# Two ordering edges in the gemm pairs of a gated streaming-encoder block: sums of the next pair's weights behind y22, the cast of its first weights behind the copy of x12

## The chip, the cores and the metric

The kernel runs on one core of a Trainium2 chip. The metric is the device time of one execution in microseconds (us), smaller being better; the time shown is the median of three runs. In the profile PE is TensorE (matmuls), PEld its weight loads, DVE is VectorE, ACT ScalarE, POOL GpSimd and SP SyncE, the engine that issues most of the DMAs. "SPq" is SP's DMA queue.

## The reference, cut to what matters

One layer, 1024 tokens of width 1024, all in float32. The change touches the first matrix product only, the input projection; everything behind it reads what that writes.

```python
D_MODEL = 1024
BATCH = 1
SEQ = 1024
DEPTH = 1
...
h = rmsnorm(x, norm_g[l])
proj = h @ w_in[l]
q, k, v, za, u, vs, zs, gm = jnp.split(proj, IN_SPLITS, axis=-1)
q = partial_rope(q.reshape(B, S, ATT_HEADS, HEAD_DIM), pos)
k = partial_rope(k.reshape(B, S, ATT_KV_HEADS, HEAD_DIM), pos)
...
a = window_sink_attention(q, k, v, att_sinks[l])
a = (a * jax.nn.silu(za)) @ w_att_out[l]
sgo = chunked_spatial_gating(jax.nn.gelu(u, approximate=False),
                             jax.nn.gelu(vs, approximate=False),
                             sg_w[l], sg_b[l], sg_ln_g[l], sg_ln_b[l])
sgo = (sgo * jax.nn.silu(zs)) @ w_sg_out[l]
ga, gs = jnp.split(jax.nn.sigmoid(gm + b_merge[l]), N_BRANCHES, axis=-1)
y = ga * a + gs * sgo
x = x + y @ w_o[l]
return rmsnorm(x, final_g)
```

## The kernel before, in words

**A product.** A float32 product is made from two halves of each factor: a "hi" in the rounded type fp32r and a "lo", the rest. `split` makes them: ScalarE casts the hi (L189), VectorE subtracts it from the source for the lo (L190). `product` then runs hi·hi, hi·lo and lo·hi for each of four blocks of the inner dimension: 12 matmuls of 128x512 into one bank (L410). The lo of a weight is therefore wanted by the third matmul of the product that uses it.

**A gemm pair.** The columns of the weights are worked off in pairs of 128-column blocks. `gemm_pair` makes one pair's result, four quarters of 128x512, from seven products in place of eight, with sums of the weights and of the activations in the factors. The forms of the activations (b11, t1, t2, b21, t3, b22, t4) are made once per stage; the forms of the weights are made for each pair:

- the first weights, unit (n, 0), of which only 512 columns are cast in pairs 0 to 5;
- the sums sa, units (n, 2) and (n, 3), two additions (L299, L300) of raw weights on VectorE, then a cast and a lo over 1024 columns;
- the sums sb, units (n, 4) and (n, 5), two more additions (L296, L297), then the same;
- the last weights, unit (n, 6).

The products are written in the order b11, t1, t2, b21, t3, b22, t4; the scheduler puts some matmuls of b22 ahead of t3. For pairs 0 to 5 (`IN_HEAD`) the b21 product is made earlier, in the head of the kernel, and written to DRAM (`made_dr`); `split_next` loads it into the free half of the first weights' hi buffer (`wh`), and VectorE adds it at L447 in place of a product. Until L447 has run, that buffer is not free.

Between the products the bank of b11, t2, t3 and t4 (`ps_mm`) and the bank of t1 and b22 (`ps_o`) are read out:

- x11 is ScalarE's copy of b11 (L444), and L447 completes it;
- x22 begins with ScalarE's negated copy of t1 (L458), which empties `ps_o` for b22;
- x12 is ScalarE's copy of the bank behind t2 (L461); t3 goes on in the same bank;
- y22 is x22 less the bank behind t3 (VectorE, L473); t4 goes on in the bank behind it;
- x12 is completed by the bank of b22 (VectorE, L477);
- the last quarter is ScalarE's copy of the bank behind t4.

`finish` sends each quarter on. Pairs 0 to 3 make U, pair 4 the keys and values, pairs 5 to 8 the queries Q. In the Q pairs each quarter is split again (`split_q`: ScalarE's L1344, VectorE's two L1346, called a qhl pair in the prediction) and stored on SP as `q_hl` (L1349), and its raw value as `q_raw` (L571). Pair 4's values go through a transpose and a cast and lo of `vt` (ScalarE, VectorE).

**Where the weights of the next pair come from.** `split_next`, called four times in a pair, takes the next unit of a list. It runs one pair ahead: the first weights of pair n+1 are cast, its sums made and its loads asked for while pair n is multiplied. Raw weights come through three `wr` buffers, hi and lo through three `wh` and `wl` buffers each, sums through two `s` buffers. A pair needs two raw buffers; each is loaded by DMAs on SP's queue (`copy_to`, L241), in the Q pairs four of 128 KB for each buffer. A load waits until the last reader of the buffer's old content is done, and what stands behind it on SP waits as well.

**What sets the order.** The program is written in one sequence; a scheduler then lays each engine's instructions in one row, following the data and its own costs, and an engine works off its row in order. `after(second, first)` adds an edge that only orders two instructions in that row: on one engine, it costs no semaphore. `make_sums(first)` passes such an edge to the first addition of each sum, where one is given; `behind_of` holds it by pair and has no entry for pairs 1 to 6 before the change.

Of the kernel before, what the change touches and what calls it, by code (L numbers as in the profile page):

```python
# [54 lines left out]
def hybrid_tile(  # L55
# [16 lines left out]
    nc = tc.nc  # L72
# [109 lines left out]
    def split(hi, lo, src, minus=False):  # L182
        if minus:
            nc.scalar.mul(hi, src, -1.0)
            return nc.vector.scalar_tensor_tensor(
                lo, src, -1.0, hi.bitcast(F32), op0=ALU.mult, op1=ALU.subtract
            )
        else:
            hi_casts.append(nc.scalar.copy(hi, src))  # L189
            return nc.vector.tensor_sub(lo, src, hi.bitcast(F32))  # L190

    def after(second, first):

        tc.add_manual_dep(
            second.ins,
            first.ins.name,
            mybir.DependencyInfo(mybir.DependencyClass.NoSync, mybir.DependencyReason.DATA),
            reason="order",
        )
# [49 lines left out]
    def split_next(hold=False):  # L249

        if not units:
            begin_job()
        if not units:
            return
        halves, keys = units.pop(0)
        if keys[0][1] == 2 and not locked[0]:
            make_sums(behind_of.get(keys[0][0]))
        if callable(halves):
            halves = halves()
        hi = mtile([P, D], F32R, "wh", 3)  # L260
        lo = mtile([P, D], F32R, "wl", 3)
        if isinstance(halves, list):
            for c, half in enumerate(halves):
                split(hi[:, half_of(c)], lo[:, half_of(c)], half)
        else:
            wide = halves.shape[1]
            if hold:
                nc.scalar.copy(hi[:, 0:wide], halves)
                for c, key in enumerate(keys):
                    ready[key] = hi[:, half_of(c)], lo[:, half_of(c)]  # L270
                return lambda: nc.vector.tensor_sub(lo[:, 0:wide], halves, hi[:, 0:wide].bitcast(F32))
            first = split(hi[:, 0:wide], lo[:, 0:wide], halves)
            splits.append(first)
            if keys[0] == (done[0] - 1, 6) and done[0] > LAST_OF_Q + 2 and not locked[0]:
                make_sums(first)
        for c, key in enumerate(keys):
            ready[key] = hi[:, half_of(c)], lo[:, half_of(c)]
        n = keys[0][0]
        if keys == [(n, 0)] and n in IN_HEAD:
            ready[n, 1] = hi[:, HALF:D].bitcast(F32)  # L280
            copy_to(ready[n, 1], made_dr[n])
        if len(units) == 1 and not locked[0]:
            begin_job()
# [22 lines left out]
        return [lambda at=at: made[at][:] for at in range(2)]  # L306

    loads_of = []
    IN_HEAD = range(6)

    def make_sums(first=None, most=2):
# [116 lines left out]
    def mark(copy):  # L428
        if not by_products[0]:
            pace[0] = copy  # L430

    def gemm_pair(b, finish, hook=lambda: None, second="o", begun=None, last_form=None):

        n = done[0]
        done[0] += 1
        if begun:
            acc = begun.pop(0)
        else:  # L440
            acc = bank("mm")[:]
            product(acc, ready[n, 0], b["b11"], True)
        x11, x12, x22 = xtile(), xtile(), xtile()
        mark(nc.scalar.copy(x11[:], acc))  # L444

        def first_term(t2):
            term[0] = nc.vector.tensor_add(x11[:], x11[:], t2)  # L447
            finish(0, 0, x11, x11[:], 1.0)

        if n in IN_HEAD:  # L450
            first_term(ready[n, 1])
        hook()
        if begun:
            t5 = begun.pop(0)
        else:
            t5 = bank("o")[:]
            product(t5, ready[n, 2], b["t1"], True)
        mark(nc.scalar.mul(x22[:], t5, -1.0))  # L458
        hook()
        product(acc, ready[n, 3], b["t2"], False)  # L460
        mark(nc.scalar.copy(x12[:], acc))  # L461
        split_next()
        hook()
        if n not in IN_HEAD:
            t2 = bank(second)[:]
            product(t2, ready[n, 1], b["b21"], True)
            first_term(t2)
        split_next()
        if last_form:
            last_form()  # L470
        hook()
        product(acc, ready[n, 4], b["t3"], False)
        term[0] = nc.vector.tensor_sub(x22[:], x22[:], acc)  # L473
        finish(1, 1, x22, x22[:], 1.0)
        hook()
        product(t5, ready[n, 5], b["b22"], False)
        term[0] = nc.vector.tensor_add(x12[:], x12[:], t5)  # L477
        finish(0, 1, x12, x12[:], 1.0)
        split_next()
        hook()  # L480
        product(acc, ready[n, 6], b["t4"], False)
        finish(1, 0, xtile(), acc, -1.0)
        split_next()
        hook()
# [755 lines left out]
    for m in range(0, KC, 2):  # L1240
        last_u[0] = m == KC - 2

        def finish(i, half, q, src, sign, m=m):
            nc.scalar.activation(q[:], src, AF.Gelu, scale=sign)
            late.append(lambda: mix(m + i, half, q))
# [215 lines left out]
    keys = {}  # L1461
# [968 lines left out]
```

## Time and profile before

| | before |
|---|---|
| device time, median of 3 runs | 900.67 us (897.28, 900.67, 901.84) |
| the profiled execution, device time | 894.7 us |
| its span in the profile | 892.3 us |
| granted TensorE clock, mean | 0.997 |
| ScalarE busy | 559.4 us (63%) |
| GpSimd busy | 164.4 us (18%) |
| DMA | 216.99 MB, mean 243 GB/s |
| HBM, read and written | 280 GB/s over the span |

TensorE's and VectorE's rows stand in the prediction. The profiled execution is one of its own, 6.0 us below the median of the timed runs; the span is the time from its first to its last recorded instruction.

In a row of the timeline the columns are: start in us from the beginning of the span, duration in us, engine, line, operation, output<-inputs (names without their buffer numbers), shapes and types, and in brackets the idle time of the engine just before, with what ended it. In the list of waits a row gives engine, tile and line of the one that waits, engine, tile and line of the one that releases it, then the sum of the idle time, the count, and the mean. In a table of windows a row gives the stretch, its length, then for PE, PEld, DVE, ACT, POOL and SP the busy time with its count, then the mean granted clock, the busy share of the DMA engines and the GB/s that they moved.

### The profile page before, as it was taken

The numbers are of one execution on the slowest core, as the hardware profiler recorded it, in microseconds if no ns is written. First come the engines' busy times: TensorE is split into PE (matmuls) and PEld (weight loads), VectorE is DVE, ScalarE is ACT, GpSimd is POOL, SyncE is SP. The second block draws the span as 40 slices with busy tenths as digits, with TensorE's granted clock in tenths as the row PEclk, the third lists the DMA queues.
The fourth block names the chain that finished last, engine by engine and source line by source line (L and its number), as shares of the span: only waits on it lengthen the run. The fifth ranks groups of instructions, "written<-read, shape, count | busy, mean of one in ns | idle before, by whom it ended". The sixth has DMA issues, their size and how long they took to land.

```text
span 892.3 us, 13261 instructions
## 1 busy us (share of the span) xinstructions
PE 882.3 (99%) x4131; PEld 731.1 (82%) x4131; DVE 698.0 (78%) x1354; ACT 559.4 (63%) x1097; POOL 164.4 (18%) x267
## 2 busy tenths in 40 slices
PE   9999999999999999999999999999999999999996
PEld 5888888887888888888888888888888888888885
DVE  7876697764687779888889887654898699579986
ACT  7775564333455468889888886443585485467543
POOL 3112311123021012323322210122201111110013
PEclk9999999999999999999999999999999999999998
DMA  9977867769788879999999994889869568998533
GB/s 326 230 205 205 210 143 172 184 213 279 254 284 264 275 238 249 262 339 278 269 340 295 269 285 127 307 302 261 229 186 358 191 193 266 284 261 274 184 123 114
DMA packets 134630, 216.99 MB, mean 243 GB/s; under 512 B 13372, under 2 KB 62144, under 8 KB 134560
## 3 DMA queue, kind: packets, MB, share of 16 engines
q1 hardware_dynamic: 111736, 152.50, 52.8%
q0 software_dynamic: 22672, 63.45, 29.4%
q8 instruction: 33, 0.54, 0.2%
q14 instruction: 37, 0.30, 0.1%
q10 hardware_dynamic: 152, 0.20, 0.1%
HBM read 157.77 MB, written 91.88 MB: 280 GB/s over the span
## 4 chain that ended last, share of the span: by engine, by line
PE 96%; DMA 2%; issue 1%; DVE 1%; SPq 0%; DVEq 0%; ACT 0%; ACTq 0%; POOLq 0%
PE ps_mm L410 46%; PE ps_o L410 25%; PE ps_tp L410 4%; PE ps_sc L410 3%; PE ps_sc L716 3%; PE ps_o L716 2%; PE ps_two L1584 2%; PE ps_tp L1214 2%; PE ps_o L1721 2%; PE ps_tp L1659 2%; PE ps_mm L716 2%; PE ps_tp L716 1%; PE ps_o L1729 1%; DMA wr<-in_x_dram 1%; PE ps_tp L1671 1%
## 5 line engine op out<-in xcount | busy, mean ns | idle before, releaser
L189 ACT CAST wh<-s 128x1024 fp32r<-128x1024 f32 (+1 forms) x66 | 65.7, 998 | 68.5 <-issue 22.1
L190 DVE TENSOR_TENSOR wl<-wr,wh 128x512 fp32r<-128x512 f32 (+1 forms) x63 | 56.0, 890 | 64.8 <-ACT wh L189 62.5
L189 ACT CAST wh<-wr 128x512 fp32r<-128x512 f32 (+1 forms) x63 | 49.2, 782 | 59.0 <-PE ps_mm L410 32.4
L190 DVE TENSOR_TENSOR wl<-s,wh 128x1024 fp32r<-128x1024 f32 (+1 forms) x66 | 76.1, 1155 | 9.4 <-ACT wh L189 8.6
L362 POOL DMA_DIRECT2D sums<-in_w_dram x48 | 35.1, 737 | 170.7 <-PE ps_mm L410 94.1
L410 PE MATMUL ps_o<-T_b22h,wh 128*128 128x512 f32 x148 | 58.2, 394 | 0.9 <-ACT x L458 0.9
L410 PE MATMUL ps_o<-T_t1h,wh 128*128 128x512 f32 x148 | 58.5, 396 | 0.0
L410 PE MATMUL ps_o<-T_t1h,wl 128*128 128x512 f32 x148 | 57.9, 391 | 0.0
L410 PE MATMUL ps_o<-T_b22h,wl 128*128 128x512 f32 x148 | 57.8, 391 | 0.0
L410 PE MATMUL ps_o<-T_t1l,wh 128*128 128x512 f32 x148 | 57.7, 390 | 0.0
L410 PE MATMUL ps_o<-T_b22l,wh 128*128 128x512 f32 x148 | 57.7, 390 | 0.0
L1631 ACT ACTIVATE pr<-pr,sm 128x193 f32<-128x193 f32 (+2 forms) x128 | 55.9, 439 | 1.7 <-DVE sm L1615 1.0
L410 PE MATMUL ps_mm<-T_t4h,wh 128*128 128x512 f32 (+1 forms) x144 | 56.4, 392 | 0.0
L410 PE MATMUL ps_mm<-T_t3h,wh 128*128 128x512 f32 x140 | 55.7, 398 | 0.0
L410 PE MATMUL ps_mm<-T_t4h,wl 128*128 128x512 f32 (+1 forms) x144 | 55.5, 385 | 0.0
L410 PE MATMUL ps_mm<-T_t4l,wh 128*128 128x512 f32 (+1 forms) x144 | 55.4, 385 | 0.0
L410 PE MATMUL ps_mm<-T_b11h,wh 128*128 128x512 f32 x140 | 55.0, 392 | 0.0
L410 PE MATMUL ps_mm<-T_t3h,wl 128*128 128x512 f32 x140 | 54.7, 391 | 0.0
L410 PE MATMUL ps_mm<-T_t3l,wh 128*128 128x512 f32 x140 | 54.7, 390 | 0.0
L410 PE MATMUL ps_mm<-T_b11l,wh 128*128 128x512 f32 x140 | 54.7, 390 | 0.0
L410 PE MATMUL ps_mm<-T_b11h,wl 128*128 128x512 f32 x140 | 54.6, 390 | 0.0
L410 PE MATMUL ps_mm<-T_t2h,wl 128*128 128x512 f32 x140 | 54.6, 390 | 0.0
(512 smaller groups left out, 2537.0 us busy)
## 6 DMA issues: line engine op xcount, KB each, us to landing
wr<-in_w_dram SPq DMA_DIRECT2D x80, 256.0 KB
sums<-in_w_dram POOLq DMA_DIRECT2D x24, 512.0 KB, 6.2
s<-sums SPq DMA_DIRECT2D x24, 512.0 KB
q_hl<-qhl SPq DMA_DIRECT2D x16, 512.0 KB
q<-q_hl SPq DMA_DIRECT2D x64, 128.0 KB
wr<-in_w_dram SPq DMA_DIRECT2D x15, 512.0 KB
y_dr<-x POOLq DMA_DIRECT2D x28, 256.0 KB, 6.1
sums<-in_w_dram POOLq DMA_DIRECT2D x24, 256.0 KB, 7.1
```

Of the source, the lines that this page charges most:

```text
L189: hi_casts.append(nc.scalar.copy(hi, src))
L190: return nc.vector.tensor_sub(lo, src, hi.bitcast(F32))
L362: return lambda: paced(nc.gpsimd.dma_start(dst, src, accum_op=op))
L410: mm = nc.tensor.matmul(acc, lt, rt, start=fresh and k == 0 and n == 0, stop=k == 3 and n == 2, skip_group_check=True,)
L716: mm = nc.tensor.matmul(acc, lt, rt, start=first and n == 0, stop=last and n == 2, skip_group_check=True)
L1214: nc.tensor.matmul(pm[:, t * P : (t + 1) * P], xh[:, half * 4 + t, g * P : (g + 1) * P], bias[-1][1][:, g % 2, :], start=True, stop=True,)
L1584: nc.tensor.matmul(st.sc[:, i], q_of[:, c, i * P : (i + 1) * P], kt[:, :, lo:hi], start=True, stop=True)
L1631: nc.scalar.activation(v, v, AF.Exp, bias=st.nmax[:, c, i : i + 1], scale=-1.0, accum_out=st.sums[:, c, i : i + 1])
L1659: nc.tensor.transpose(st.inner[0 : P if st.t else 64, at : at + P], st.pr[:, i, place_of(c, 64 if st.t else P, 192)], ident[:],)
L1671: nc.tensor.transpose(st.ends[0:wide, i * P : (i + 1) * P], st.pr[:, i, 129 : 129 + wide], ident[:])
L1721: nc.tensor.matmul(st.po[:], lt, rt, start=i == 0, stop=False, skip_group_check=True)
L1729: nc.tensor.matmul(st.po[:, cols(c)], ends[:, c, vs], st.b[:, cols(c)], start=False, stop=c == 1, skip_group_check=True)
```

## The change: what it does

Three edits, all of order; no instruction is added or taken away.

1. In `split_next`, the cast of pair n+1's first weights is ordered behind pair n's copy of x12 (L461), if that copy was kept.
2. In `gemm_pair`, that copy is kept in `copies` for pairs 0 to 5.
3. In `gemm_pair`, y22's subtraction (L473) of pairs 0 to 5 is put into `behind_of` for the next pair, so that the four additions of pair n+1's sums are ordered behind it.

```diff
@@ split_next
             first = split(hi[:, 0:wide], lo[:, 0:wide], halves)
+            if keys[0][1] == 0 and keys[0][0] - 1 in copies:
+                after(hi_casts[-1], copies[keys[0][0] - 1])
             splits.append(first)
@@
     loads_of = []
+    copies = {}
     IN_HEAD = range(6)
@@ gemm_pair
         product(acc, ready[n, 3], b["t2"], False)
-        mark(nc.scalar.copy(x12[:], acc))
+        second_copy = nc.scalar.copy(x12[:], acc)
+        mark(second_copy)
+        if n in IN_HEAD:
+            copies[n] = second_copy
         split_next()
@@
         product(acc, ready[n, 4], b["t3"], False)
         term[0] = nc.vector.tensor_sub(x22[:], x22[:], acc)
+        if n in IN_HEAD:
+            behind_of[n + 1] = term[0]
         finish(1, 1, x22, x22[:], 1.0)
```

The lines behind the edits move down: L447 is L450 after the change, L458 L461, L461 L464, L473 L479, L477 L485, the additions L299, L300, L296, L297 are L301, L302, L298, L299, and L1344, L1346, L1349, L571 are L1352, L1354, L1357, L579, and L410 L413.

Below are the rows at three places, before and after, as the program lays them (line, operation, output<-inputs, shape; the first number in a name counts tiles).

VectorE, from the end of pair 4 to y22 of pair 5, before. `s_321` and `s_322` are the sums of pair 6, made of its raw weights `wr_305` and `wr_306`; `s_299` is the first sum of pair 5; `x_310` is x11, `x_312` x22 of pair 5; `wh_293` holds the product made in the head for it.

```order
L190 TENSOR_TENSOR khl_297_1935<-x_287_1846,khl_297_1935 128x512
L299 TENSOR_TENSOR s_321_2095<-wr_306_1972 128x512
L190 TENSOR_TENSOR wl_304_1968<-s_299_1945,wh_303_1967 128x1024
L300 TENSOR_TENSOR s_321_2095<-s_321_2095,wr_305_1971 128x512
L296 TENSOR_TENSOR s_322_2098<-wr_305_1971,wr_306_1972 128x512
L190 TENSOR_TENSOR vt_308_1986<-ps_tp_307_1981,vt_308_1986 128x8x64
L447 TENSOR_TENSOR x_310_2011<-x_310_2011,wh_293_1891 128x512
L297 TENSOR_TENSOR s_322_2098<-wr_305_1971,s_321_2095 128x512
L190 TENSOR_TENSOR wl_316_2050<-wr_282_1804,wh_315_2049 128x512
L190 TENSOR_TENSOR wl_318_2054<-wr_305_1971,wh_317_2053 128x1024
L1346 SCALAR_TENSOR_TENSOR qhl_313_2017<-x_310_2011,qhl_313_2017 128x256 x2
L473 TENSOR_TENSOR x_312_2013<-x_312_2013,ps_mm_309_1998 128x512
```

VectorE after, the same place up to the last lo ahead of y22.

```order
L190 TENSOR_TENSOR khl_297_1935<-x_287_1846,khl_297_1935 128x512
L190 TENSOR_TENSOR wl_304_1968<-s_299_1945,wh_303_1967 128x1024
L190 TENSOR_TENSOR vt_308_1986<-ps_tp_307_1981,vt_308_1986 128x8x64
L450 TENSOR_TENSOR x_310_2011<-x_310_2011,wh_293_1891 128x512
L190 TENSOR_TENSOR wl_316_2050<-wr_282_1804,wh_315_2049 128x512
L190 TENSOR_TENSOR wl_318_2054<-wr_305_1971,wh_317_2053 128x1024
```

And the rows that follow these, from y22 (L479 now) to the lo of pair 6's first sum, `wl_324`; `qhl_319` is the split of y22, `qhl_320` that of x12 (`x_311`).

```order
L479 TENSOR_TENSOR x_312_2013<-x_312_2013,ps_mm_309_1998 128x512
L301 TENSOR_TENSOR s_321_2095<-wr_306_1972 128x512
L1354 SCALAR_TENSOR_TENSOR qhl_313_2017<-x_310_2011,qhl_313_2017 128x256 x2
L1354 SCALAR_TENSOR_TENSOR qhl_319_2071<-x_312_2013,qhl_319_2071 128x256 x2
L485 TENSOR_TENSOR x_311_2012<-x_311_2012,ps_o_314_2022 128x512
L302 TENSOR_TENSOR s_321_2095<-s_321_2095,wr_305_1971 128x512
L298 TENSOR_TENSOR s_322_2098<-wr_305_1971,wr_306_1972 128x512
L1354 SCALAR_TENSOR_TENSOR qhl_320_2090<-x_311_2012,qhl_320_2090 128x256 x2
L299 TENSOR_TENSOR s_322_2098<-wr_305_1971,s_321_2095 128x512
L190 TENSOR_TENSOR wl_324_2102<-s_321_2095,wh_323_2101 128x1024
```

All four additions have moved from ahead of L473 (three of them from ahead of L447) to behind it; pair 5's own `wl_304` and the `vt` of pair 4 have moved up.

ScalarE in pair 5, before; `wh_315` is the hi of pair 5's last weights, `wh_317` that of pair 6's first weights, `wh_323` that of pair 6's first sum, `x_311` x12.

```order
L444 COPY x_310_2011<-ps_mm_309_1998 128x512
L189 CAST wh_315_2049<-wr_282_1804 128x512
L458 ACTIVATE x_312_2013<-ps_o_314_2022 128x512
L189 CAST wh_317_2053<-wr_305_1971 128x1024
L461 COPY x_311_2012<-ps_mm_309_1998 128x512
L1344 ACTIVATE qhl_313_2017<-x_310_2011 128x4x2x64
```

And after:

```order
L447 COPY x_310_2011<-ps_mm_309_1998 128x512
L189 CAST wh_315_2049<-wr_282_1804 128x512
L461 ACTIVATE x_312_2013<-ps_o_314_2022 128x512
L464 COPY x_311_2012<-ps_mm_309_1998 128x512
L189 CAST wh_317_2053<-wr_305_1971 128x1024
L1352 ACTIVATE qhl_313_2017<-x_310_2011 128x4x2x64
```

One swap: the cast of `wh_317` now stands behind the copy of x12.

TensorE at the same place, from the last matmul of t2 to the first of t3, before. `ps_o_314` is the bank of t1 and b22 in pair 5, `ps_mm_309` the other; `wh_303` and `wl_304` are pair 5's second sum.

```order
L410 MATMUL ps_mm_309_1998<-T_t2h_128_708,wl_301_1949 128x512
L410 MATMUL ps_o_314_2022<-T_b22h_79_448,wh_303_1967 128x512
L410 MATMUL ps_o_314_2022<-T_b22l_80_449,wh_303_1967 128x512
L410 MATMUL ps_o_314_2022<-T_b22h_79_448,wl_304_1968 128x512
L410 MATMUL ps_o_314_2022<-T_b22h_79_448,wh_303_1967 128x512
L410 MATMUL ps_o_314_2022<-T_b22l_80_449,wh_303_1967 128x512
L410 MATMUL ps_o_314_2022<-T_b22h_79_448,wl_304_1968 128x512
L410 MATMUL ps_o_314_2022<-T_b22h_79_448,wh_303_1967 128x512
L410 MATMUL ps_mm_309_1998<-T_t3h_138_792,wh_303_1967 128x512
```

And after:

```order
L413 MATMUL ps_mm_309_1998<-T_t2h_128_708,wl_301_1949 128x512
L413 MATMUL ps_o_314_2022<-T_b22h_79_448,wh_303_1967 128x512
L413 MATMUL ps_o_314_2022<-T_b22l_80_449,wh_303_1967 128x512
L413 MATMUL ps_o_314_2022<-T_b22h_79_448,wl_304_1968 128x512
L413 MATMUL ps_o_314_2022<-T_b22h_79_448,wh_303_1967 128x512
L413 MATMUL ps_mm_309_1998<-T_t3h_138_792,wh_303_1967 128x512
```

Three of the seven b22 matmuls ahead of t3 have moved behind it; four stay. In pairs 1 and 3 one moves so, in pair 4 two.

SP from the loads of pair 7 on, before; `wr_329` and `wr_330` are pair 7's raw buffers, `qhl_313`, `qhl_319`, `qhl_320` and `qhl_326` the four quarters of pair 5.

```order
L241 DMA wr_329_2129<-in_w_dram 128x2x128 x4
L241 DMA wr_330_2130<-in_w_dram 128x2x128 x4
L1319 DMA rot_335_2156<-in_cos_dram 128x128
L1320 DMA rot_335_2156<-in_sin_dram 128x128
L1349 DMA q_hl_95<-qhl_313_2017 128x2x512
L571 DMA q_raw_94<-x_312_2013 128x512
L571 DMA q_raw_94<-x_311_2012 128x512
L1349 DMA q_hl_95<-qhl_319_2071 128x2x512
L1349 DMA q_hl_95<-qhl_320_2090 128x2x512
L571 DMA q_raw_94<-x_325_2117 128x512
L1349 DMA q_hl_95<-qhl_326_2120 128x2x512
```

And after:

```order
L241 DMA wr_329_2129<-in_w_dram 128x2x128 x4
L1327 DMA rot_335_2156<-in_cos_dram 128x128
L1328 DMA rot_335_2156<-in_sin_dram 128x128
L579 DMA q_raw_94<-x_312_2013 128x512
L1489 DMA v_488_3075<-v_dr_98 64x2x192
L1357 DMA q_hl_95<-qhl_313_2017 128x2x512
L1357 DMA q_hl_95<-qhl_319_2071 128x2x512
L579 DMA q_raw_94<-x_311_2012 128x512
L1357 DMA q_hl_95<-qhl_320_2090 128x2x512
L579 DMA q_raw_94<-x_325_2117 128x512
L1357 DMA q_hl_95<-qhl_326_2120 128x2x512
L241 DMA wr_330_2130<-in_w_dram 128x2x128 x4
```

The four loads of `wr_330` have moved from behind those of `wr_329` to behind the last store of pair 5.

## The prediction

> **What bounds the kernel now.** First the page's totals, the clock and the chain that ended last.
>
> ```profile
> span 892.3 us, 13261 instructions
> PE 882.3 (99%) x4131; PEld 731.1 (82%) x4131; DVE 698.0 (78%) x1354; ACT 559.4 (63%) x1097; POOL 164.4 (18%) x267
> PEclk9999999999999999999999999999999999999998
> PE 96%; DMA 2%; issue 1%; DVE 1%; SPq 0%; DVEq 0%; ACT 0%; ACTq 0%; POOLq 0%
> ```
>
> TensorE is the bound: 99% busy, at full granted clock, 96% of the chain. An edit that moves only vector, scalar and DMA work can gain what TensorE waits, or cost new waits, and nothing else. So the second view is the waits of TensorE alone, over the whole span; this is all of it.
>
> ```profile
> PE ps_o L629 <- DVE T_b22l L117: 1.5, 1, 1.5
> PE ps_o L410 <- ACT x L458: 0.9, 1, 0.9
> PE ps_mm L811 <- ACT T_t2h L735: 0.6, 1, 0.6
> ```
>
> Two of the three lie in the first 13 us, ahead of all gemm pairs. One, 0.9 us, lies among the pairs that the diff touches. The timeline places it: first TensorE around it.
>
> ```profile
> 212.85 0.39 PE L410 MATMUL ps_o<-T_t1h,wh 128*128 128x512 f32 x1
> ...
> 217.38 0.39 PE L410 MATMUL ps_mm<-T_t2h,wl 128*128 128x512 f32 x1
> 218.62 0.50 PE L410 MATMUL ps_o<-T_b22h,wh 128*128 128x512 f32 x1 [0.86 <-ACT x L458]
> ...
> 224.39 0.50 PE L410 MATMUL ps_mm<-T_t4h,wh 128*128 128x512 f32 x1
> 224.73 0.40 PE L410 MATMUL ps_mm<-T_t4l,wh 128*128 128x512 f32 x1
> ```
>
> This is pair 5, the first Q pair. From 212.85 to 217.38 are 20 steps, so a step is 0.2265 us. After its t2 product TensorE stands until ScalarE has read t5 (L458). ScalarE and VectorE tell why it is late.
>
> ```profile
> 208.91 1.05 ACT L189 CAST wh<-s 128x1024 fp32r<-128x1024 f32 x1 [0.71 <-PE ps_mm L410]
> ...
> 211.21 0.59 ACT L189 CAST vt<-ps_tp 128x512 fp32r<-128x512 f32 x1 [0.74 <-PE ps_tp L1286]
> 212.35 0.59 ACT L444 COPY x<-ps_mm 128x512 f32<-128x512 f32 x1 [0.56 <-PE ps_mm L410]
> 217.46 0.62 ACT L189 CAST wh<-wr 128x512 fp32r<-128x512 f32 x1 [4.51 <-DVE x L447]
> 217.98 0.59 ACT L458 ACTIVATE x<-ps_o 128x512 f32<-128x512 f32 x1
> 218.47 1.04 ACT L189 CAST wh<-wr 128x1024 fp32r<-128x1024 f32 x1
> 219.41 0.59 ACT L461 COPY x<-ps_mm 128x512 f32<-128x512 f32 x1
> ```
>
> ```profile
> 204.21 0.69 DVE L473 TENSOR_TENSOR x<-x,ps_mm 128x512 f32<-128x512 f32 x1 [2.86 <-PE ps_mm L410]
> ...
> 213.19 0.69 DVE L299 TENSOR_TENSOR s<-wr 128x512 f32<-128x512 f32 x1 [3.91 <-DMA wr<-in_w_dram]
> 213.80 1.22 DVE L190 TENSOR_TENSOR wl<-s,wh 128x1024 fp32r<-128x1024 f32 x1
> 214.94 0.68 DVE L300 TENSOR_TENSOR s<-s,wr 128x512 f32<-128x512 f32 x1
> ...
> 216.74 0.68 DVE L447 TENSOR_TENSOR x<-x,wh 128x512 f32<-128x512 f32 x1
> ...
> 223.66 0.68 DVE L473 TENSOR_TENSOR x<-x,ps_mm 128x512 f32<-128x512 f32 x1
> ```
>
> VectorE sat 3.91 us at the first sum of pair 6 (L299), whose weights had not landed. Behind it stood L447 of pair 5, which frees the wh buffer for ScalarE's cast at 217.46, which stands ahead of L458. So TensorE's wait comes from a sum that nobody needed yet.
>
> **The change, part by part.** Instructions are the same in kind and number; only order changes.
>
> *The sums of pair 6 go behind y22 (L473) of pair 5.* Then, from these rows: VectorE's lo part of s (1.14 a step) follows the cast that ends at 209.96, and ends by 211.2; that of vt follows its cast and ends at 212.4; L447 follows the copy that ends at 212.94, and is done at 213.6 instead of 217.4. The cast takes 0.62, and L458 then waits only for t1's end, about 215.1: done at 215.7, and TensorE asks at 217.38 + 0.23 = 217.61. The 0.86 us is gone, with 1.9 us to spare. What is late next is the x12 copy (L461): t3 needs it.
>
> *The cast of pair 6's first weights goes behind that copy.* The copy then starts when t2 ends, 217.38 + 0.39, and ends at about 218.4; four b22 matmuls, which the new order leaves ahead of t3, cover until 217.61 + 4 × 0.2265 = 218.52. No wait, 0.1 us spare. The moved cast (1.04) is done by 219.4 and wanted at 225.8. In pairs 0 to 4 the same swap has no wait of TensorE to remove (the list above is complete), and the casts have spare time of the same kind: I count them at nothing. If the copy's cover is gone, a pair loses about 0.1 us.
>
> The sums of pairs 2 and 5 move as well, and their products come later still.
>
> ```profile
> 144.07 0.69 DVE L473 TENSOR_TENSOR x<-x,ps_mm 128x512 f32<-128x512 f32 x1 [2.27 <-PE ps_mm L410]
> 153.89 0.39 PE L410 MATMUL ps_o<-T_t1h,wh 128*128 128x512 f32 x1
> ```
>
> From L473 at 144.07, four steps of 0.60 (the third is L477), a mixing step of 0.67, the cast of 1.05 and the lo of 1.2 end by 149.4; t1 of pair 2 starts at 153.89. For pair 5 the same count from 204.21 ends by 209.6; its t1 starts at 212.16, three steps ahead of 212.85. Both cost nothing; if that cover were gone, each would cost the 1.2 of its lo.
>
> *The gain.* From 217.38 to 224.39 TensorE makes 25 steps in 7.01 us; at 0.2265 they take 5.66. TensorE's start of t4 had also to wait for L473 at 223.66, so its first step took 0.34 for 0.23: in all **1.45 us**.
>
> *What the moved sums release later.* Each raw buffer is read by sums and then refilled on SP's queue, so its loads move too.
>
> ```profile
> 203.49 4.32 SPq L241 DMA_DIRECT2D wr<-in_w_dram  x5
> 218.83 5.95 SPq L241 DMA_DIRECT2D wr<-in_w_dram  x8
> 226.04 0.38 SPq L1349 DMA_DIRECT2D q_hl<-qhl  x1
> 207.20 5.43 DMA wr<-in_w_dram
> 229.16 0.67 ACT L1344 ACTIVATE qhl<-x 128x512 fp32r<-128x512 f32 x1 [0.34 <-DMA q_hl<-qhl]
> 250.36 0.36 SPq L1349 DMA_DIRECT2D q_hl<-qhl  x1
> ```
>
> The fourth row is from the chain: the last load of the group of five landed 5.43 us after its issue at 207.20, and its sum started at 213.19, 6.0 after. The fifth gives 3.1 us from the issue of a store at 226.04 to its first user. These are my two ends, from issue to use.
>
> Pair 6's second buffer now waits for the last sum of pair 5. Behind L473 at 204.21 come six steps of 0.60, so that sum ends at 208.5; two small stores go out first, then four loads of 0.86, the last at 211.5: in use by 217.5 at the latest, and its sum stands at 221.9. Hidden, 4 us spare. From there VectorE's queue (the order in front shows it; steps of 0.60, 0.67 for a qhl pair, 1.14 for a lo) reaches the lo of pair 6's first s at 227.0 to 228.2. t1 of pair 6 wants it at 217.61 + 48 × 0.2265 + 0.45 = 228.9. Hidden, 0.7 us spare.
>
> Pair 7's second buffer is the tight one. Its four loads went out in the eight from 218.83; now they stand on SP behind four stores of q_hl, the last of which waits for VectorE: after 228.2 a small copy, a lo and a qhl pair, so 230.1. Four issues of 0.74: the last at 232.8, in use from 235.9 or 238.8. VectorE's sums of pair 7 wait for it, and they are not held behind anything: ahead of L447 and L473 of pair 6 they stand as they did before at pair 5. VectorE is held until 235.2 anyway, by a lo whose cast waits for t2. TensorE's next starts of t4 are:
>
> ```profile
> 244.49 0.39 PE L410 MATMUL ps_mm<-T_t4h,wh 128*128 128x512 f32 x1
> 263.53 0.39 PE L410 MATMUL ps_mm<-T_t4h,wh 128*128 128x512 f32 x1
> ```
>
> Pair 6's t4 needs L473, and is due at 244.49 - 1.45 = 243.04. From the first use, three sums, L447, a sum, a lo, a qhl pair and L473 take 1.8 + 0.6 + 0.6 + 1.14 + 0.67 + 0.69 = 5.5: L473 ends at 241.4 or 244.3. A wait of 0 or **1.3 us**; it begins with a first use after 237.5. To choose, the bytes in that stretch:
>
> ```profile
> q_hl<-qhl SPq DMA_DIRECT2D x9, 512.0 KB
> wr<-in_w_dram SPq DMA_DIRECT2D x24, 128.0 KB
> q_raw<-x SPq DMA_DIRECT2D x9, 256.0 KB
> 225.00:235.00 10.00, 10.00 (x46) 8.27 (x45) 8.23 (x21) 4.77 (x8) 0.00 (x0) 1.00 0.92 329
> 235.00:245.00 10.00, 10.00 (x50) 8.29 (x49) 5.00 (x9) 4.91 (x8) 0.00 (x0) 1.00 0.59 184
> ```
>
> Four q_hl, four q_raw and the four loads are 3.67 MB; at 329 GB/s (the last column of the first stretch) 11.2 us from 222.5, so 233.7, ahead of the last issue plus 3.1. I take the lower end, no wait, and keep 1.3.
>
> The Trainium skill, DMA: Bandwidth & Descriptors, section Anatomy of one DMA, fits one copy at about 2.0 us plus bytes over 436 GB/s, 2.3 us for 128 KB. By that the last load lands at 235.1 and the sum stays 1.45; by the row's 5.43 and the 0.56 behind it the gain is all but lost. The trace has 5.43 where the page would have 2.3.
>
> Pair 8's last load goes behind pair 7's last q_hl store in the same way: issued at 250.36 + 0.36 - 1.45 = 249.3, in use from 252.4 or 255.3. From there four sums and a short lo, L447, a rotation, a lo, a qhl pair, a rotation and L473 (3.0 + 0.6 + 0.6 + 1.14 + 0.67 + 0.6 + 0.69) take 7.3: L473 of pair 7 ends at 259.7 or 262.6, and t4 is due at 263.53 - 1.45 = 262.08: 0 or **0.5 us**, and again I take the lower end. After that the orders agree but for one step.
>
> *The sum.* 892.3 - 1.45 = 890.85 of span; the profiled execution, with the 2.4 us around its span, goes from 894.7 to 893.25. The median of the three timed runs is 900.67, 6.0 above the profiled one; less 1.45 it is **899.2**. With both upper ends, 1.8, the sum is +0.35 and the median 901.0.
>
> **The rivals.** *The wait moves to pair 6 (slower).* If pair 7's loads come later than the rows say, the same stall is made anew: each us after 237.5 is one lost, and from 238.95 on the change loses. For it: the five loads took 213.19 - 203.49 = 9.7 us from first issue to use; 9.7 from 230.6 is 240.3, a wait of 2.8. Pair 8's load, 1.5 us later than its upper end in the same way, adds 0.5 + 1.5 = 2.0. Sum -1.45 + 4.8 = +3.35: 904.0. Against it: they ran against POOL's stores of k and v, and the two stretches above have none (POOL 0.00), the second with the DMA engines 0.59 busy. [...]
>
> *The gain is larger.* Timed runs lie 2.6 to 7.1 us above the profiled one (897.28 and 901.84 against 894.7). Where a load lands later, the old order loses one for one and the new has 4 us spare. If a third of the median's 6.0 is this wait, the gain is 3.5: 897.2. Against it: nothing shows where those 6 us are.
>
> *The change does not do what it says.* L447 still comes after 216.2, since something else holds VectorE, and L458 with it: 900.7. The rows above leave 2.6 us against that.
>
> **How the numbers follow.** Forecast 899.2 (its own range 899.2 to 901.0): 0.66. Slower, 904.0: 0.14. Larger gain, 897.2: 0.13. No effect, 900.7: 0.07. The range goes from the fastest run less the gain, 897.28 - 1.45 = 895.8, to 902.9, half way from the slowest run with no gain, 901.84, to the slower rival; half of that rival and the far tail of the larger gain stay outside. About what a measurement of this kernel can tell from no change is 0.5%, 4.5 us: below 896.2 only by the tail of the larger gain, 0.06; above 905.2 only by a landing far beyond the rival's, 0.04; the rest 0.90.
>
> **What would show it.** Right: TensorE's list of waits has no L458; L447 of pair 5 starts near 213.0; ScalarE's copy L461 of pair 5 near 217.8; t4 of pair 6 near 243.0. Wrong: a wait of TensorE on y22 in pairs 6 or 7, VectorE idle at the first sum of pair 7 beyond 237.5, a wait on the x12 copy in any pair, or TensorE's time lost in a stretch that no moved row touches.

## The result: 893.5 us, and a profile that hardly moved

| | before | after |
|---|---|---|
| device time, median of 6 runs each | 900.36 us (896.12 to 901.84) | 893.47 us (892.65 to 893.88) |
| ratio after to before | | 0.993, 95% interval 0.9906 to 0.9955 |
| the profiled execution, device time | 894.7 us | 893.83 us |
| its span | 892.3 us | 892.0 us |

The change makes the kernel 6.9 us faster by the medians, about 6 us by the ratio (0.7% of 900, 0.45 to 0.94%). The forecast was 899.2 with a range from 895.8: too little by 5.7 us, and the time lies outside the range. Yet the spans of the two profiles differ by 0.3 us, and the runs of after lie within 1.2 us, those of before within 5.7. The question is thus not only where the time went, but why the profile of before did not have it.

First the profile after, the page's head and TensorE's whole list of longer waits.

```profile
span 892.0 us, 13264 instructions
PE 882.1 (99%) x4131; PEld 731.1 (82%) x4131; DVE 697.6 (78%) x1354; ACT 558.9 (63%) x1097; POOL 164.4 (18%) x267
```

```profile
PE ps_o L637 <- DVE T_b22l L117: 1.5, 1, 1.5
PE ps_mm L819 <- ACT T_t2h L743: 0.7, 1, 0.7
PE ps_two L1592 <- DMA q<-q_hl: 0.6, 1, 0.6
```

The wait on t5 (L458, now L461) is gone, and none has come in the pairs behind it. The timelines after, for ScalarE, VectorE and TensorE, at the places that the prediction named:

```profile
212.25 0.59 ACT L447 COPY x<-ps_mm 128x512 f32<-128x512 f32 x1 [0.57 <-PE ps_mm L413]
213.86 0.62 ACT L189 CAST wh<-wr 128x512 fp32r<-128x512 f32 x1 [1.02 <-DVE x L450]
214.99 0.60 ACT L461 ACTIVATE x<-ps_o 128x512 f32<-128x512 f32 x1 [0.52 <-PE ps_o L413]
217.71 0.59 ACT L464 COPY x<-ps_mm 128x512 f32<-128x512 f32 x1 [2.12 <-PE ps_mm L413]
```

```profile
212.87 0.96 DVE L450 TENSOR_TENSOR x<-x,wh 128x512 f32<-128x512 f32 x1 [0.46 <-ACT x L447]
...
222.04 0.69 DVE L301 TENSOR_TENSOR s<-wr 128x512 f32<-128x512 f32 x1
...
236.88 0.69 DVE L301 TENSOR_TENSOR s<-wr 128x512 f32<-128x512 f32 x1 [1.60 <-DMA wr<-in_w_dram]
...
241.70 0.68 DVE L479 TENSOR_TENSOR x<-x,ps_mm 128x512 f32<-128x512 f32 x1
...
254.25 0.69 DVE L301 TENSOR_TENSOR s<-wr 128x512 f32<-128x512 f32 x1 [2.97 <-DMA wr<-in_w_dram]
...
260.87 0.69 DVE L479 TENSOR_TENSOR x<-x,ps_mm 128x512 f32<-128x512 f32 x1
```

```profile
243.06 0.39 PE L413 MATMUL ps_mm<-T_t4h,wh 128*128 128x512 f32 x1
...
262.10 0.39 PE L413 MATMUL ps_mm<-T_t4h,wh 128*128 128x512 f32 x1
```

All came as foreseen: x11 completed (L450) at 212.87, foreseen 213.0; the x12 copy at 217.71, foreseen 217.8; pair 6's t4 at 243.06, foreseen 243.04, against 244.49 before. So the gain of 1.4 us in this profile is real. Of it 1.2 us are lost again far behind, where no moved row lies: the start of a matmul after, less that of the same one before, goes from -1.44 at 270 us to -1.16 at 297, and from -1.13 at 500 to -0.25 at 514, where the third row of the list waits for a load of queries. In a second profile of the changed kernel (below) neither of these two is there, and its list has no such row; it loses 0.9 us at t1 of pair 6 and 0.4 near 301 us instead, and its span is 892.2. Such losses come and go between executions. The span shows three instructions more than before; none is among those counted as busy, whose counts are the same on every engine.

### The profile page after: what moved, and what is told of

It is laid out like the page before. It is cut to its first block, busy times and chain, and to the rows that moved or that the text cites. A ratio compares the mean times of both kernels' runs of the same rounds, so it can differ in the third digit from the quotient of the medians.

```text
span 892.0 us, 13264 instructions
## 1 busy us (share of the span) xinstructions
PE 882.1 (99%) x4131; PEld 731.1 (82%) x4131; DVE 697.6 (78%) x1354; ACT 558.9 (63%) x1097; POOL 164.4 (18%) x267
## 4 chain that ended last, share of the span: by engine, by line
PE 95%; DMA 4%; DVE 0%; SPq 0%; issue 0%; DVEq 0%; ACT 0%; ACTq 0%
PE ps_mm L413 45%; PE ps_o L413 25%; PE ps_tp L413 4%; PE ps_sc L413 3%; PE ps_sc L724 3%; PE ps_o L724 2%; PE ps_two L1592 2%; DMA k<-k_dr 2%; PE ps_tp L1222 2%; PE ps_mm L724 2%; PE ps_tp L1667 1%; PE ps_o L1729 1%; PE ps_tp L724 1%; DMA q<-q_hl 1%; DMA wr<-in_x_dram 1%; PE ps_o L1737 1%
## 5 line engine op out<-in xcount | busy, mean ns | idle before, releaser
L413 PE MATMUL ps_o<-T_t1h,wh 128*128 128x512 f32 x148 | 58.6, 396 | 0.0
L413 PE MATMUL ps_o<-T_b22h,wh 128*128 128x512 f32 x148 | 58.0, 392 | 0.0
L413 PE MATMUL ps_o<-T_b22h,wl 128*128 128x512 f32 x148 | 57.9, 392 | 0.0
L413 PE MATMUL ps_o<-T_t1h,wl 128*128 128x512 f32 x148 | 57.9, 391 | 0.0
L413 PE MATMUL ps_o<-T_t1l,wh 128*128 128x512 f32 x148 | 57.7, 390 | 0.0
L413 PE MATMUL ps_o<-T_b22l,wh 128*128 128x512 f32 x148 | 57.7, 390 | 0.0
L413 PE MATMUL ps_mm<-T_t4h,wh 128*128 128x512 f32 (+1 forms) x144 | 56.3, 391 | 0.0
L413 PE MATMUL ps_mm<-T_t3h,wh 128*128 128x512 f32 x140 | 55.7, 398 | 0.0
L413 PE MATMUL ps_mm<-T_t4l,wh 128*128 128x512 f32 (+1 forms) x144 | 55.5, 385 | 0.0
L413 PE MATMUL ps_mm<-T_t4h,wl 128*128 128x512 f32 (+1 forms) x144 | 55.4, 385 | 0.0
L413 PE MATMUL ps_mm<-T_b11h,wh 128*128 128x512 f32 x140 | 55.0, 393 | 0.0
L413 PE MATMUL ps_mm<-T_t3l,wh 128*128 128x512 f32 x140 | 54.8, 391 | 0.0
L413 PE MATMUL ps_mm<-T_t3h,wl 128*128 128x512 f32 x140 | 54.7, 391 | 0.0
L413 PE MATMUL ps_mm<-T_b11l,wh 128*128 128x512 f32 x140 | 54.6, 390 | 0.0
L413 PE MATMUL ps_mm<-T_t2h,wh 128*128 128x512 f32 x140 | 54.6, 390 | 0.0
L413 PE MATMUL ps_mm<-T_t2h,wl 128*128 128x512 f32 x140 | 54.6, 390 | 0.0
```

Source lines behind the costliest of these rows:

```text
L413: mm = nc.tensor.matmul(acc, lt, rt, start=fresh and k == 0 and n == 0, stop=k == 3 and n == 2, skip_group_check=True,)
```

## The experiments

**Where are the 6 us? The kernel before, profiled again.** No edit.

> The kernel before, unchanged, profiled a second time. Theory A (one wait that varies): the profiled execution of before was one with an early landing; in most executions the weights of pair 6 land later, and TensorE's wait on L458 in pair 5 is longer, one for one. Then this profile's device time is about 892.5 plus what pair 5 loses: at a median run of 900.4 the wait of L458 is about 7 us, not 0.9, and the idle time of VectorE ahead of the first sum of pair 6 is about 10 us, not 3.9. Theory B (the time is lost elsewhere): a profile of 900 shows a wait of about 1 us at L458, and the other 5 to 6 us in other waits or in slower matmuls.

This execution took 901.26 us, with a span of 899.4; the ten runs of this kernel here lie between 893.9 and 903.97. Its list of TensorE's waits begins so:

```profile
PE ps_o L410 <- ACT x L458: 6.1, 1, 6.1
PE ps_o L629 <- DVE T_b22l L117: 1.5, 1, 1.5
```

It is the same wait, seven times as long. VectorE and TensorE there:

```profile
218.36 0.69 DVE L299 TENSOR_TENSOR s<-wr 128x512 f32<-128x512 f32 x1 [9.19 <-DMA wr<-in_w_dram]
...
221.91 0.68 DVE L447 TENSOR_TENSOR x<-x,wh 128x512 f32<-128x512 f32 x1
```

```profile
217.26 0.39 PE L410 MATMUL ps_mm<-T_t2h,wl 128*128 128x512 f32 x1
223.79 0.80 PE L410 MATMUL ps_o<-T_b22h,wh 128*128 128x512 f32 x1 [6.15 <-ACT x L458]
224.39 0.63 PE L410 MATMUL ps_o<-T_b22l,wh 128*128 128x512 f32 x1
...
227.80 0.43 PE L410 MATMUL ps_mm<-T_t3h,wl 128*128 128x512 f32 x1
228.07 0.40 PE L410 MATMUL ps_mm<-T_t3h,wh 128*128 128x512 f32 x1
```

The weights of pair 6 came 5.2 us later than in the first profile (218.36 against 213.19), though they were asked for at the same time (the five loads begin at 203.60 against 203.49). The wait grew from 0.86 to 6.15, and there is a second price that was not expected: behind it, from 224.39 to 227.80, eight steps take 3.41 us, 0.43 each in place of 0.2265. From 217.26 to 228.07 TensorE loses 8.3 us (11 steps at 0.2265 would take 2.5), where the first profile lost 1.45.

That the profile of before was one of the short waits is seen in the timed runs as well. Of the 35 runs of before that stood beside the first four experiments, 16 took 893.8 to 896.7 us with a mean granted clock of 0.997 to 0.999, and 19 took 897.4 to 903.0 with 0.993 to 0.996. The first profile of before has 0.997 and the second 0.995, so the lower clock is read here as the mark of the long wait. The split is not always so clean: of the 69 runs of before beside the later experiments, 11 took 897.1 to 901.0 us at 0.997, and no run of that kind was profiled. The changed kernel's 14 runs, these 6 and 8 further down, all have 0.997 to 0.999.

**Which part of the change? The sums alone, the casts alone, pair 6's sums alone.** The first has only this edit:

```diff
         term[0] = nc.vector.tensor_sub(x22[:], x22[:], acc)
+        if n in IN_HEAD:
+            behind_of[n + 1] = term[0]
```

The second has the rest of the change without it (against the changed kernel):

```diff
-        if n in IN_HEAD:
-            behind_of[n + 1] = term[0]
```

The third is the first for one pair:

```diff
         term[0] = nc.vector.tensor_sub(x22[:], x22[:], acc)
+        if n == 5:
+            behind_of[n + 1] = term[0]
```

> The sums of pairs 1 to 6 ordered behind y22, the casts left as before. Theory A: all of the gain, 893.5 us give or take 1, ratio to before 0.992, and a spread of the runs of about 1 us. Theory B (the casts ahead of the copy of x12 cost the rest): 1.4 us of it, 899, ratio 0.998, with the spread of before.

> The casts of the first weights ordered behind the copy of x12, the sums left as before. Theory A: no gain, about 900, the spread of before (5 us). Theory B: most of the gain, about 895.

> Only pair 6's four sums ordered behind y22 of pair 5; the order of TensorE stays that of before, row by row. Theory A: all of the gain, 893.5 us give or take 1, spread about 1 us. Theory C (each of the six pairs gives a part of it in the timed runs): about 899, one or two us below before.

| | median | runs | ratio to before, 95% interval |
|---|---|---|---|
| sums alone | 894.49 us | 893.28 to 895.26 | 0.9946, 0.9927 to 0.9964 |
| casts alone | 902.67 us | 900.7 to 904.28 | 1.0056, 1.0034 to 1.0078 |
| pair 6's sums alone | 894.39 us | 892.56 to 895.33 | 0.996, 0.9939 to 0.9982 |

Pair 6's four sums carry the gain; the other pairs' sums add nothing that shows. The casts alone are slower than before, which neither theory expected. The profile has the long wait, and the times and clocks (0.992 to 0.995) of all 12 runs point to it. VectorE and TensorE in the casts' profile:

```profile
217.41 0.69 DVE L301 TENSOR_TENSOR s<-wr 128x512 f32<-128x512 f32 x1 [9.21 <-DMA wr<-in_w_dram]
```

```profile
PE ps_o L413 <- ACT x L461: 6.2, 1, 6.2
```

**Through which instruction? The sums behind L447 only.** They stay ahead of y22, and no other engine's order changes.

```diff
         if n in IN_HEAD:
             first_term(ready[n, 1])
+        if n == 5:
+            behind_of[6] = term[0]
```

> Before, with pair 6's four sums ordered behind L447 of pair 5 only: they stay ahead of y22 (L473), and nothing moves on TensorE, ScalarE, GpSimd or SP. Theory A1 (the loss goes through L447, the cast behind it and L458): all of the gain, 894 us give or take 1, no wait on L458; y22 is due only near 221.5, and the weights have landed by 218.4 at the latest. Theory A2 (y22 being held matters as much): 1 us or more stays, and shows as a wait ahead of t4 of pair 5.

894.06 us (893.0 to 897.24), ratio 0.9943 (0.9918 to 0.9968). VectorE:

```profile
213.58 0.69 DVE L447 TENSOR_TENSOR x<-x,wh 128x512 f32<-128x512 f32 x1 [0.46 <-ACT x L444]
216.97 0.69 DVE L299 TENSOR_TENSOR s<-wr 128x512 f32<-128x512 f32 x1 [2.70 <-DMA wr<-in_w_dram]
...
222.87 0.69 DVE L475 TENSOR_TENSOR x<-x,ps_mm 128x512 f32<-128x512 f32 x1
```

The weights come late here too, at 216.97, and it costs nothing at L458; y22 (L475 here) was held a little, 0.2 us by the list of waits. In a kernel without the change's casts, then, it is enough that L447 is not held.

**Casts and L447 together.** The changed kernel, with the sums of pair 6 alone held, behind L450 (L447 before) in place of y22:

```diff
             first_term(ready[n, 1])
+        if n == 5:
+            behind_of[6] = term[0]
...
-        if n in IN_HEAD:
-            behind_of[n + 1] = term[0]
```

> The casts as in the changed kernel, and of the sums only pair 6's held, behind L447's successor of pair 5 (L450) and not behind y22. If the mechanism is L447 alone, 892.5 to 893.5, as the changed kernel, with no wait of TensorE on a lo at t1 of pair 6 (0.6 us in one profile of the changed kernel), since the lo of pair 6's first sum is done some 2 us earlier; a wait on y22 ahead of t4 of pair 5 of about 0.2 us, as with L447 alone. If holding them behind y22 matters: 895 or more.

898.44 us (895.58 to 901.43), ratio 0.9991 (0.9967 to 1.0014): some 5 us worse than the changed kernel, which the expectation had only for the case that y22 matters. VectorE, and TensorE's wait:

```profile
212.10 0.69 DVE L450 TENSOR_TENSOR x<-x,wh 128x512 f32<-128x512 f32 x1 [0.46 <-ACT x L447]
...
219.20 0.69 DVE L301 TENSOR_TENSOR s<-wr 128x512 f32<-128x512 f32 x1 [6.40 <-DMA wr<-in_w_dram]
...
223.48 0.68 DVE L481 TENSOR_TENSOR x<-x,ps_mm 128x512 f32<-128x512 f32 x1
```

```profile
PE ps_mm L413 <- DVE x L481: 1.8, 1, 1.8
```

With the casts the weights came late in both profiles (219.20 here, 217.41 with the casts alone), and here the sums then hold y22, and with it t4, in place of L447. So with the casts it does matter that the sums stand behind y22; without them it was enough to stand behind L447.

**Why does the load land late?** The suspect is contention. In the two profiles of before, the DMA queues between 213 us, when the load has landed in the first, and 218.2, when it lands in the second (packets, MB, share of the 16 engines). The first profile:

```profile
DMA packets 339, 1.07 MB, mean 207 GB/s; under 512 B 76, under 2 KB 76, under 8 KB 339
q0 software_dynamic: 332, 1.07, 63.7%
q1 hardware_dynamic: 7, 0.01, 0.3%
```

And the second:

```profile
DMA packets 436, 1.15 MB, mean 221 GB/s; under 512 B 93, under 2 KB 157, under 8 KB 436
q0 software_dynamic: 334, 1.09, 60.6%
q1 hardware_dynamic: 102, 0.06, 3.8%
```

GpSimd's stores of k_dr and v_dr (the software queue) are nearly the same. What differs is 0.05 MB on SP's queue: the last rows of the load (512 bytes each: 157 less 93, 64 packets, where the first profile has none) and the small k_raw stores. They trickle in beside GpSimd's stores; from 217 us on, when those are done, the last 43 packets of SP's queue follow one another, and the load is in use at 218.36. The Trainium skill, DMA: Bandwidth & Descriptors, section Queues, rings and completion order, says that each DMA engine takes turns between the queues it has work for, a packet at a time, and that one copy is spread over up to 16 engines; the load would then be as late as the busiest of them, which agrees with the trickle, but the trace does not name the engines.

The kernel with the casts alone fits too. The order of GpSimd's row changed a little in it, and the second group of stores to k_dr begins 4.6 us after the first of the five loads (203.93), in place of 6.1 (203.49). Before, and with the casts alone:

```profile
209.58 2.43 POOL L1276 DMA_DIRECT2D k_dr<-khl  x4 [1.23 <-DVE khl L190]
208.50 2.43 POOL L1282 DMA_DIRECT2D k_dr<-khl  x4 [1.00 <-DVE khl L190]
```

The kernel with the casts and L447 has the same 208.50. That this is why the load lands late there was not tested by itself. Three kernels were to test the contention. Two copy 1 MB more from DRAM to DRAM on GpSimd's queue behind the first v_dr store, one in before, one in the changed kernel:

```diff
+            if half == 1:
+                for i in range(2):
+                    extra = nc.gpsimd.dma_start(extra_dr[i], w[W_U + i])
+                    after(extra, stored)
+                    stored = extra
```

> Before, with 1 MB more copied from DRAM to DRAM on GpSimd's queue right behind the first v_dr store; the output does not use it. Theory A with contention (the weights of pair 6 land when the backlog of GpSimd's stores on the DMA engines is gone): 2 MB moved at some 330 GB/s are 6 us more backlog, the first sum of pair 6 starts up to 6 us later than 213 to 218, TensorE's wait in pair 5 is 7 to 12 us, and the time 901 to 908 in all runs. If the landing does not hang on GpSimd's stores: as before, 894 to 902.

> The changed kernel with the same 1 MB more. The sums stand behind y22 (222.0) and have the whole backlog up to there hidden, so of the 6 us only what lies behind 222 can cost: 893.5 to 896, no wait on L461 in pair 5, and a spread of 1 to 2 us. If the change only wins because the landing is early in it: as late as its counterpart, 900 or more.

The third keeps GpSimd's stores of v_dr and of the second half of k_dr in a list and lets them wait for L458 of pair 5:

```diff
+        taken = nc.scalar.mul(x22[:], t5, -1.0)
+        mark(taken)
+        while n == 5 and held:
+            paced(held.pop(0)(), taken)
```

> Before, order of the sums untouched (they stand ahead of L447), but GpSimd's stores of v_dr and of the second half of k_dr wait until ScalarE has read t5 in pair 5 (L458), so that nothing of GpSimd's runs beside the loads of pair 6. If their contention makes the landing late: the first sum of pair 6 starts by 212, L447 by 215, and TensorE does not wait at L458 in pair 5, in all runs; the time is 893 to 896 unless the later stores hold something else. If it is something else in the load: the wait stays, 1 to 6 us.

| | median | runs | first sum of pair 6 starts |
|---|---|---|---|
| before, 1 MB more | 903.61 us | 900.76 to 905.67 | 217.96 |
| changed, 1 MB more | 896.59 us | 895.19 to 900.85 | 222.03 |
| before, stores held back | 903.65 us | 902.21 to 904.93 | 214.01 |

With 1 MB more, no run of before took less than 900.76 us, where 21 of the 31 plain runs beside it did, and the ten clocks are 0.992 to 0.996: all have the long wait by these signs, and the profile shows it (5.2 us). Up to that wait no engine's order differs from before but for the added copies. In the profile the landing is at the late end, not 6 us beyond it: the size of that expectation was wrong. The changed kernel keeps 7 us of distance, but pays more for the extra traffic than was expected, with a spread of 5.7 us: at 222.03 its sum still waited 0.62 us for the load, off TensorE's path, and TensorE lost 1.0 us on y22 of pair 7.

```profile
262.89 0.50 PE L414 MATMUL ps_mm<-T_t4h,wh 128*128 128x512 f32 x1 [1.02 <-DVE x L480]
```

That loss is not a later load: the first sum of pair 8 starts at 254.32, against 254.25 in the changed kernel. The scheduler laid VectorE's row in another order here from 222.6 us on, with two more instructions between that sum and y22, which starts at 262.15 against 260.87. So this kernel's time does not measure the 1 MB alone.

With the stores held back, the DMA engines stand idle from 214 to 218 and the first sum starts at 214.01, yet not by 212, and TensorE still waits 1.3 us at L458. GpSimd's queue was not empty in that kernel: loads of `sums` asked for at 205.1 were not held, and it moved 0.40 MB between 207 and 213. From the end of the last issue to the first sum are 6.0 us there, against 5.4 and 10.6 in the two profiles of before and 9.2 with 1 MB more. So the order of before waits a little even without those stores. That the stores make up the difference agrees with the trickle and with the 1 MB; it is not shown beyond that, and why the same kernel has 5.4 in one execution and 10.6 in another stays open. That kernel loses its time at another place: the stores now meet the loads of pair 7, whose eight issues take 11.5 us on SP in place of 5.95, and TensorE stands 5.1 us at the rotation tables.

**What are the casts worth, and are the later pairs at risk?** On one chip the changed kernel again, the sums alone again, and the changed kernel with the sums of pairs 7 and 8 held too:

```diff
-        if n in IN_HEAD:
+        if n < 8:
             behind_of[n + 1] = term[0]
```

> The changed kernel again, beside the next two on the same chip. Theory A: 892.5 to 895, nothing waits in pair 5. It is the measure for the casts: if they are worth something once the sums are moved, it is below the kernel with the sums alone by 0.5 us or more.

> The kernel with the sums of pairs 1 to 6 moved and the casts left alone, again, beside the changed kernel on the same chip. If the casts are worth nothing by themselves: within 0.5 us of the changed kernel. If they gave part of the gain: 0.5 to 1.5 us above it.

> The changed kernel, with the sums of pairs 7 and 8 held behind y22 of pairs 6 and 7 too, where VectorE still sat 1.6 and 3.0 us at a first sum in the profile after. The prediction's two terms there (0 or 1.3 us, 0 or 0.5 us) were taken as 0. If that is right in all runs, this is within 0.5 us of the changed kernel; if timed runs lose something there, it is 0.5 to 1.8 us faster, with a smaller spread; if the later sums come too late for t1 of the next pair, it is slower, with a wait there.

892.69 us (891.98 to 894.23), 894.49 (892.41 to 896.49) and 893.26 (892.51 to 894.21); ratios to before 0.9924, 0.9944 and 0.9933. Holding pairs 7 and 8 gives nothing that shows: the two terms taken as 0 are 0. The casts give 1.8 us on top of the sums here, or 1.2 by the third kernel, which has them as well. A part of it can be read: from t1 of pair 2 to t1 of pair 5, before

```profile
153.89 0.39 PE L410 MATMUL ps_o<-T_t1h,wh 128*128 128x512 f32 x1
...
212.16 0.40 PE L410 MATMUL ps_o<-T_t1h,wh 128*128 128x512 f32 x1
```

and after

```profile
154.01 0.39 PE L413 MATMUL ps_o<-T_t1h,wh 128*128 128x512 f32 x1
...
212.05 0.39 PE L413 MATMUL ps_o<-T_t1h,wh 128*128 128x512 f32 x1
```

58.27 us become 58.04. The eight profiles with the casts unmoved have 58.24 to 58.29, the six with the casts moved 57.98 to 58.04. So the casts gain 0.23 us in three pairs, none of it a wait long enough for the list. A second part lies in pair 6. From t1 of pair 5 to t4 of pair 6 the two profiles with the sums alone take 32.13 and 32.04 us; the changed kernel takes 31.01 and 31.87, and 30.93 with pairs 7 and 8 held too. The list of the first profile with the sums alone has two waits at t1 of pair 6 for it:

```profile
PE ps_o L410 <- DVE wl L190: 0.3, 1, 0.3
PE ps_o L410 <- ACT wh L189: 0.2, 1, 0.2
```

Where the rest is stays open; single profiles differ by as much at the start of the kernel and in the attention.

A thin place showed as well. TensorE in the second profile of the changed kernel, at t1 of pair 6:

```profile
229.71 0.50 PE L413 MATMUL ps_o<-T_t1h,wl 128*128 128x512 f32 x1 [0.59 <-DVE wl L190]
```

## Why the prediction was right about the mechanism and wrong about the time

- **The bound and the wait** (TensorE at 99%, the wait at L458 made by a sum that nobody needed yet): right; the sums of pair 6 alone and those held behind L447 alone each remove the wait and give the gain.
- **The gain in the profiled execution, 1.45 us**: right, 1.43 by pair 6's t4 (244.49 to 243.06). The span was forecast at 890.85 and measured 892.0, with the 1.2 us that this execution lost far behind.
- **The sum is the step that failed.** It took the gain of one execution, 1.45, off the median of others, 6.0 us above it. The wait of 0.86 us was the short end of one that varies: 6.15 us in the second profile, and 8.3 us lost with the slow matmuls behind it. On what the runs show, the term is 1.45 us in one execution and 8.3 in another, and 6.9 between the medians. The rival "the gain is larger" had the mechanism, a landing that costs the old order one for one, but gave it a third of the 6.0 and a chance of 0.13. "Nothing shows where those 6 us are" was its counterargument; yet the quoted list had only one wait among the gemm pairs, and it hung on a DMA beside other traffic, so that was the place to look first.
- **The half-speed matmuls** were in no term, and "can gain what TensorE waits ... and nothing else" left them out: 2.0 us in the second profile (ten steps from 223.79 to 228.07 took 4.28, at 0.2265 they take 2.27).
- **The spare time of the new order** (weights used up to 222 without loss): right; it is why the runs of after lie within 1.2 us. Even with 1 MB more the first sum waited 0.62 us for its weights, off TensorE's path.
- **Pairs 7 and 8** (0 or 1.3, 0 or 0.5; taken as 0): right. First uses were at 236.88 and 254.25, within 235.9 to 238.8 and 252.4 to 255.3, and y22 ended 0.7 and 0.5 us ahead of t4.
- **t1 of pair 6, 0.7 us spare**: mis-sized. One profile of the changed kernel waits 0.59 there and loses 0.9 in all, another does not.
- **The casts, counted at nothing**: mis-sized. They gain 0.23 us in pairs 2 to 4, and 1.2 to 1.8 us in the time once the sums are moved; alone they come with a late landing. Why is open: GpSimd's earlier stores fit, but were not tried by themselves.
- **The slower rival**: it did not happen, and no run here shows it. With 1 MB more TensorE did wait for y22 of pair 7, but the load behind it was no later.
- One statement ahead of the prediction was wrong: `behind_of` does have entries for pairs 1 to 4 before the change (statistics at L1166 and L1178, the mixing product at L1230). The sums of pairs 1, 3 and 4 stood behind y22 already; only those of pairs 2, 5 and 6 moved.

## What to carry to other kernels

When the profiled execution is faster than all timed runs, and the runs spread by more than the profile's wait, look for a wait in it that ends on a transfer beside other traffic, and price it at its late end too. A second profile of the same kernel can show it: here it did, though 16 of the 35 runs above had the short wait. An instruction that waits for a transfer should not stand ahead of one that another engine needs sooner; move it behind, as far as its own user allows, and the spread goes with the mean. Two order edits can each move the other's margin: L447 was enough alone, and not with the casts.

## What was not expected of the hardware

**A wait of TensorE is paid twice once it is long enough.** The windows of two microseconds of the second profile of before (columns as in the tables ahead; the granted clock is the third from the right):

```profile
218.00:220.00 2.00, 0.00 (x0) 0.00 (x0) 1.64 (x2) 0.00 (x0) 0.00 (x0) 1.00 0.00 0
220.00:222.00 2.00, 0.00 (x0) 0.00 (x0) 2.00 (x5) 0.00 (x0) 0.00 (x0) 0.76 0.00 0
222.00:224.00 2.00, 0.21 (x1) 0.21 (x2) 1.88 (x3) 1.38 (x3) 0.77 (x1) 0.50 0.28 102
224.00:226.00 2.00, 2.00 (x5) 1.61 (x6) 1.23 (x1) 1.16 (x2) 0.00 (x0) 0.50 0.96 347
226.00:228.00 2.00, 2.00 (x6) 1.52 (x5) 0.00 (x0) 0.57 (x1) 0.62 (x2) 0.53 0.92 241
```

TensorE stood from 217.6; the clock fell to 0.50 near 221 (0.76 over that window), and came back just before 228, some 4 us after work began at 223.79. In the casts' profile TensorE stood from 216.9, the clock fell near 218.9, 2.0 us later, and came back near 229.2, 6.1 us after work began at 223.09. Half clock lasted 6.8 us here, 10.2 there and 3.4 in the profile below. Waits of 5.1, 5.2, 6.1 and 6.2 us in these profiles show it; those of 0.9, 1.0 and 1.3 do not. But one of 1.8 does, that of casts and L447 together, from 222.4 to 224.21:

```profile
222.00:224.00 2.00, 0.41 (x2) 0.00 (x0) 2.00 (x3) 0.43 (x1) 0.70 (x2) 1.00 0.47 138
224.00:226.00 2.00, 1.79 (x5) 1.44 (x6) 1.93 (x6) 1.60 (x2) 0.00 (x0) 0.70 0.70 195
226.00:228.00 2.00, 2.00 (x6) 1.59 (x5) 2.00 (x4) 0.68 (x1) 0.00 (x0) 0.50 0.77 239
```

There the clock fell after work had begun again. The Trainium skill, TensorE: Matmul & The Clock Gate, part 1, puts the fall at an idle window of about 3.4 us and the return at about 3.4 us of work at half rate. The fall in the first five rows agrees, 3.4 us after TensorE stopped. The 2.0 us in the casts' profile and the wait of 1.8 us are shorter than such a window, and the measurement decides: in this kernel one wait of 1.8 us cost the slow matmuls too, and one of 1.3 did not. The returns came 4.0 to 6.1 us after work began in these three.

**A load can land up to 5 us later with nothing changed**: issued at the same time, beside the same stores, in use at 213.19 in one execution and at 218.36 in another.
